# Attention's fill work in a decoder layer: key and value pieces ahead of query pieces, latents loaded one pair per unit, VectorE splitting the key and value weights

## The chip, the cores and the metric

The kernel runs on one core of a Trainium2 chip. The metric is the device time of one execution in microseconds (us); the median of three runs is compared. A profiled execution has a time of its own and a span, from its first to its last instruction.

## The reference, cut to what matters

One layer of a hybrid decoder on 1024 tokens of width 1024, all in float32. A combined input projection feeds two attention mixers and two gates; their gated sum goes through an output projection, then a SwiGLU follows. The mixers have eight heads each:

```python
y_a = _dilated_attention(a_qkv, rel_bias) @ w_up_a            # mixer A, heads 0 to 7
# mixer B: latents c_q (768) and c_kv (256), normalised, expanded per head
q  = einsum('bsl,lhd->bshd', _rmsnorm(c_q,  g_q_lora),  w_uq)   # 8 heads x (64 + 32)
kv = einsum('bsl,lhd->bshd', _rmsnorm(c_kv, g_kv_lora), w_ukv)  # 8 heads x (64 + 64)
q_nope, q_rope = q[..., :64], _rope(q[..., 64:], positions)
k_nope, v = kv[..., :64], kv[..., 64:];  k_rope = _rope(k_r, positions)
# causal softmax((q_nope k_nope + q_rope k_rope) * scale) v
merged = sigmoid(gate_a) * y_a + sigmoid(gate_b) * (y_b @ w_up_b)
```

The expansions with w_uq, w_ukv and w_up_a are the work that the change reorders.

## The kernel before

Every float32 matrix is kept as a rounded high part and the remainder as a low part, and a product is three matmuls (high times high, high times low, low times high). Making the two parts is a "split": ScalarE casts the high part (line L83), then VectorE or GpSimd subtracts it from the source (L84). `wsplit` does that for the weights of mixer B.

The attention stage follows the input projection (whose matmuls are L220). It is a loop over 64 units: unit u is two blocks of 128 queries of head u // 4, the eight heads of mixer A first. A unit's scores are matmuls (L783) that VectorE reads (L785), ScalarE exponentiates (L790) and normalises (L793, or VectorE at L795); three units later its probabilities are transposed (L805), split into ph and pl (L83, L84) and multiplied with v (L824). The next head's q, k0, k1 and v are loaded on GpSimd's DMA queue (L744 to L746 and L748) and its bias table on SyncE's (L747), once the head before the current one has given its buffers back.

Between the units' matmuls TensorE gets fill work from a generator: `spend` hands out matmuls in proportion to the attention work issued. Up to unit 32 the generator is `fill_a`. Its pieces write one accumulator, tile `acc`, which has one buffer:

- f_uk1, eight key pieces of six matmuls (L892), split into two tiles and stored to mkd (L336, L337);
- f_vb, eight value pieces of six matmuls (L87 to L89), copied to SBUF (L939), split into two tiles of which each is stored to vbd (L944);
- f_uq, twelve query pieces of 18 matmuls (L892). Four of them are rotated (L843 to L848), with two table loads `ev<-cst` each.

The tiles of all of them are called ev and come from one pool of seven buffers. `k_rope`, at unit 1, takes eight of these tiles: for each half of the tokens it loads krr (L882) and two tables (L843, L844), shuffles on VectorE (L845), multiplies and adds on GpSimd (L846 to L848), and stores the parts to krd (L884, L885).

The normalised latents lie in DRAM as nqd0 to nqd5 (query) and nqd6, nqd7 (key and value). `load_n` brings a pair of them into SBUF cells on GpSimd's queue (L874), 512 KB each. The raw weight wuk is loaded into cell 4, which later holds one half of nqd2; wuv and wuq are loaded by SyncE (L855).

A scheduler with a timeline of its own orders the instructions of each engine when the program is built. It may move an instruction ahead of others that were written before it, so the written order alone doesn't say what stands on an engine.

Of the kernel before, what the change touches and what calls it, by code (L numbers as in the profile page):

```python
# [27 lines left out]
T = 1024  # L28
# [16 lines left out]
def layer_kernel(ctx: ExitStack, tc: tile.TileContext, xT, c, pos, relT, wada, bada, gains, gq, gkv,  # L45
# [3 lines left out]
    ACT, DVE, PE, POOL, SP = nc.scalar, nc.vector, nc.tensor, nc.gpsimd, nc.sync  # L49
# [32 lines left out]
    def split(src, hi, lo, eng=DVE):  # L82
        ACT.copy(hi, src)  # L83
        eng.tensor_sub(lo, src, f32(hi))  # L84
# [316 lines left out]
    with ExitStack() as s0:  # L401
# [6 lines left out]
        ssq = [early.tile([P, H], F32, name=f"ssq{i}") for i in range(2)]  # L408
# [77 lines left out]
        for k in range(8):  # L486
# [5 lines left out]
            raw = gwr.tile([P, GW], F32, name="gwraw")  # L492
# [5 lines left out]
            hi = gwr.tile([P, GW + 32], F32R, name="gwh")  # L498
            lo = gwr.tile([P, NGP * P], F32R, name="gwl")
# [13 lines left out]
            for j in range(NGP):  # L513
                s = slice(j * P, j * P + P)
# [205 lines left out]
    with ExitStack() as s2:  # L720
# [15 lines left out]
        v_ins = [None]  # L736
# [116 lines left out]
        def wraw(src, n, t=None):  # L853
            raw = (wf.tile([P, T], F32, name="wraw") if t is None else t)[:, :n]
            ld(raw, src)  # L855
            return raw

        def wsplit(src, n, raw=None):
            raw = wraw(src, n) if raw is None else raw
            if n == T:  # L860
                hi, lo = [wk.tile([P, T], F32R, name=f"wk{l}") for l in range(2)]
            else:
                hi, lo = [wf.tile([P, 768], F32R, name=f"w{l}")[:, :n] for l in range(2)]
            split(raw, hi, lo, POOL)
            return hi, lo

        wcols = lambda w: [t.rearrange("p (k f) -> p k f", f=P) for t in w]
# [3 lines left out]
        def load_n(j):  # L871
            t = [cell(NHOME[j] + l, [P, T]) for l in range(2)]
            for l in range(2):
                ldr(t[l], nqd[j][l])  # L874
            nt[j] = t
# [3 lines left out]
        def k_rope():  # L879
            for hf in range(2):  # L880
                t = EV()
                ld(t[:32], krr[:, hsl[hf]])  # L882
                hi, lo = rope(t, 32, hf)
                st(krd[0][:, hsl[hf]], f32(hi)[:32])  # L884
                st(krd[1][:, hsl[hf]], f32(lo)[:32])  # L885
# [60 lines left out]
        def f_uk1(j, hf):  # L946
            ps = accb()
            yield from gemm3g(ps, cur["uk"], n_act(6), 2, hf, 2 * j)
            qk_out(ps, mkd[j], hf, EV)

        def fill_a():
            small = [f_uk1(j, hf) for j in range(4) for hf in range(2)] + [f_vb(tb) for tb in range(8)]
            big = [f_uq(j, hf) for j in (4, 0, 1, 5, 2, 3) for hf in range(2)]
            pat = cycle("ssq")
            while small or big:
                kind = next(pat)
                src = small if kind == "s" and small or not big else big
                yield from src.pop(0)

        def fill_b():  # L960
            for j in range(8):
# [12 lines left out]
        def open_unit(u):  # L974
# [5 lines left out]
                ld(mtab[0], maskt)  # L980
            units[u] = Unit(heads[idx], I, osum[0], 64 * (idx % 2), idx)

        def others(u):
            idx, I = u // 4, u % 4
            if I == 1 and idx < 15:
                heads[idx + 1] = load_head(*seq[idx + 1], (idx + 1) % 2)
            if u == 1:
                with tc.issue_after(v_ins[0].ins):
                    for j in (0, 1, 3, 4, 5, 2):
                        load_n(j)  # L990
                k_rope()

        DEPTH = 3
        FA, FB = (0, 0.7, 32), (35, 0.38)
# [94 lines left out]
    ssq = [X(), X()]  # L1089
# [162 lines left out]
    for ci in range(NC):  # L1252
        for dd in range(2):
# [7 lines left out]
            if dd == 1 and ci == NC - 1:  # L1261
                tail = []
                for f in (20, 21):
                    raw = cell(next(tcell), dt=F32)
                    raw = [raw[:, 0], raw[:, 1]]
# [12 lines left out]
    raw = WP.tile([P, 16, P], F32, name="Wraw")  # L1278
# [158 lines left out]
```

## Time and profile before

| | |
|---|---|
| median of 3 runs | 1672.65 us (1670.92 to 1677.95) |
| profiled execution, its own time | 1676.03 us |
| its span | 1674.2 us |
| TensorE (PE) busy | 1537.7 us, 92% of the span |
| VectorE (DVE) busy | 1240.5 us, 74% |
| ScalarE (ACT) busy | 829.8 us, 50% |
| GpSimd (POOL) busy | 561.5 us, 34% |
| moved by DMA | 321.92 MB, mean 192 GB/s |

Times in the views are microseconds from the span's start. The attention stage runs from about 440 to 838; unit 32 and the end of `fill_a` lie near 667. In a view by time, a bracket at the end of a line tells how long the engine had been idle before it and what ended that.

### The profile page before, as it was taken

The numbers are of one execution on the slowest core, as the hardware profiler recorded it, in microseconds if no ns is written. First come the engines' busy times: TensorE is split into PE (matmuls) and PEld (weight loads), VectorE is DVE, ScalarE is ACT, GpSimd is POOL, SyncE is SP. The second block draws the span as 40 slices with busy tenths as digits, with TensorE's granted clock in tenths as the row PEclk, the third lists the DMA queues.
The fourth block names the chain that finished last, engine by engine and source line by source line (L and its number), as shares of the span: only waits on it lengthen the run. The fifth ranks groups of instructions, "written<-read, shape, count | busy, mean of one in ns | idle before, by whom it ended". The sixth has DMA issues, their size and how long they took to land.

```text
span 1674.2 us, 22241 instructions
## 1 busy us (share of the span) xinstructions
PE 1537.7 (92%) x7306; PEld 1278.2 (76%) x7306; DVE 1240.5 (74%) x2433; ACT 829.8 (50%) x1631; POOL 561.5 (34%) x515
## 2 busy tenths in 40 slices
PE   4989997999779989999999998989999999899996
PEld 2758786877668778999878876768888887688775
DVE  7986669576368657989866678767777786688887
ACT  5743334444467767878733563434444443222324
POOL 0143524424244546433141134322233222222323
PEclk9989999999879999999999998999999999999997
DMA  9438457558997878766195422554454449866412
GB/s 329 178 119 310 160 188 233 172 165 251 295 223 201 202 186 206 189 164 152 46 345 171 151 100 87 178 203 167 175 187 161 152 160 353 324 247 256 154 51 101
DMA packets 175652, 321.92 MB, mean 192 GB/s; under 512 B 37020, under 2 KB 72524, under 8 KB 170288
## 3 DMA queue, kind: packets, MB, share of 16 engines
q1 hardware_dynamic: 107376, 241.75, 42.2%
q0 software_dynamic: 48000, 42.04, 11.7%
q10 hardware_dynamic: 20160, 36.71, 5.8%
q8 instruction: 58, 0.95, 0.2%
q14 instruction: 58, 0.48, 0.1%
HBM read 222.73 MB, written 102.34 MB: 194 GB/s over the span
## 4 chain that ended last, share of the span: by engine, by line
PE 43%; DVE 8%; DMA 8%; ACT 3%; issue 2%; POOL 1%; ACTq 0%; SPq 0%; DVEq 0%; POOLq 0%
PE bk L220 25%; PE acc L892 3%; PE S L783 3%; PE bk L87 3%; PE bk L88 3%; PE bk L89 3%; PE pv L824 2%; DMA Wraw<-wdown 2%; DVE Wop L84 2%; PE tr L805 2%; DMA vbd<-ev 2%; DMA tod<-x 1%; DVE x L1241 1%; DVE cell L84 1%; DMA actd<-x 1%
## 5 line engine op out<-in xcount | busy, mean ns | idle before, releaser
L220 PE MATMUL bk<-cell,Wop 128*128 128x512 f32 x4056 | 951.5, 396 | 51.5 <-DVE x L233 11.0
L220 PEld LDWEIGHTS bk<-cell,Wop 128*128 128x128 f32 x4056 | 771.8, 191 | 225.1 <-ACT x L163 15.1
L190 POOL TENSOR_TENSOR Wsum<-Wraw 128x512 f32<-128x512 f32 (+1 forms) x120 | 156.4, 1304 | 599.0 <-DVE Wop L84 272.2
L83 ACT CAST Wop<-Wsum 128x512 fp32r<-128x512 f32 (+1 forms) x241 | 130.6, 550 | 198.9 <-PE bk L220 117.3
L83 ACT CAST Wop<-Wraw 128x512 fp32r<-128x512 f32 (+2 forms) x182 | 105.6, 593 | 212.4 <-PE bk L220 75.3
L84 DVE TENSOR_TENSOR Wop<-Wsum,Wop 128x512 fp32r<-128x512 f32 (+1 forms) x241 | 155.3, 653 | 61.1 <-ACT Wop L83 60.6
L84 DVE TENSOR_TENSOR Wop<-Wraw,Wop 128x512 fp32r<-128x512 f32 (+2 forms) x182 | 152.3, 843 | 39.5 <-ACT Wop L83 35.8
L783 PE MATMUL S<-cell,cell 128*128 128x128 f32 (+8 forms) x480 | 119.3, 364 | 9.7 <-DMA cell<-ksd 5.5
L1241 DVE SCALAR_TENSOR_TENSOR x<-bk,modc,x 128x512 f32<-128x512 f32 x140 | 103.5, 744 | 20.1 <-PE bk L220 18.8
L84 DVE TENSOR_TENSOR pl<-tr,ph 128x512 fp32r<-128x512 f32 (+1 forms) x160 | 98.4, 630 | 23.9 <-ACT ph L83 22.9
L790 ACT ACTIVATE P<-P,mx 128x512 f32<-128x512 f32 (+7 forms) x128 | 99.3, 778 | 29.5 <-DVE mx L785 17.6
L892 PE MATMUL acc<-cell,w 128*128 128x512 f32 x408 | 112.0, 402 | 0.1
L190 POOL TENSOR_TENSOR Wsum<-Wraw,Wsum 128x512 f32<-128x512 f32 (+1 forms) x60 | 78.5, 1313 | 68.9 <-DVE Wop L84 66.1
L805 PE MATMUL tr<-ident,P 128*128 128x128 f32 x576 | 94.1, 281 | 5.9 <-ACT P L793 5.3
L163 ACT COPY x<-bk 128x512 f32<-128x512 f32 x92 | 52.7, 588 | 91.0 <-PE bk L220 48.1
L87 PE MATMUL bk<-cell,Wop 128*128 128x512 f32 (+1 forms) x240 | 92.3, 385 | 3.7 <-ACT Wop L83 1.9
L824 PE MATMUL pv<-ph,v 128*128 128x256 f32 (+1 forms) x320 | 88.9, 294 | 6.9 <-ACT ph L83 5.6
L783 PEld LDWEIGHTS S<-cell,cell 96*128 96x128 f32 (+1 forms) x480 | 80.8, 196 | 18.6 <-DMA cell<-ksd 5.9
L88 PE MATMUL bk<-cell,Wop 128*128 128x512 f32 (+1 forms) x240 | 91.7, 383 | 0.0
L83 ACT CAST ph<-tr 128x512 fp32r<-128x512 f32 (+1 forms) x160 | 83.3, 545 | 16.3 <-PE tr L805 13.5
L89 PE MATMUL bk<-cell,Wop 128*128 128x512 f32 (+1 forms) x240 | 90.3, 379 | 0.0
L824 PE MATMUL pv<-pl,v 128*128 128x256 f32 x320 | 83.0, 294 | 4.5 <-DVE pl L84 4.1
(255 smaller groups left out, 2221.1 us busy)
## 6 DMA issues: line engine op xcount, KB each, us to landing
tod<-x ACTq DMA_DIRECT2D x140, 256.0 KB, 2.9
cell<-tod SPq DMA_DIRECT2D x70, 512.0 KB, 6.8
Wraw<-win SPq DMA_DIRECT2D x18, 1024.0 KB, 6.6
Wraw<-wgate SPq DMA_DIRECT2D x11, 1024.0 KB, 5.5
Wraw<-wup SPq DMA_DIRECT2D x11, 1024.0 KB, 6.0
Wraw<-wdown SPq DMA_DIRECT2D x20, 512.0 KB, 6.6
ada<-wada SPq DMA_DIRECT2D x16, 512.0 KB, 6.1
cell<-ksd POOLq DMA_DIRECT2D x16, 512.0 KB, 21.4
```

The costliest lines, as they stand in the source:

```text
L83: ACT.copy(hi, src)
L84: eng.tensor_sub(lo, src, f32(hi))
L87: PE.matmul(ps, w[0], a[0], start=first, stop=False)
L88: PE.matmul(ps, w[0], a[1], start=False, stop=False)
L89: PE.matmul(ps, w[1], a[0], start=False, stop=last)
L190: POOL.tensor_tensor(t, a, b, op=op)
L220: PE.matmul(ps, w[:, wi, k], t[k][:, ti], start=start and k == 0 and n == 0, stop=k == self.nk - 1 and n == 2, skip_group_check=True)
L783: anchor[0] = PE.matmul(s, q[:, i * P:i * P + P], k[:, c * wd:c * wd + wd], start=pi == 0, stop=pi == len(passes) - 1)
L805: anchor[0] = PE.transpose(tr[:, co:co + P], self.p[a][:, kb * P:kb * P + P], ident)
L824: anchor[0] = PE.matmul(pv[:, o if l else 0:], v[:, kk], p[:, l:r], start=kk == 0 and n == 0, stop=last and l > 0 and n == 1, skip_group_c ...
L892: PE.matmul(ps, w[wi][:, k0 + k], act(k, ai, hf), start=k == 0 and n == 0, stop=k == nk - 1 and n == 2)
L1241: DVE.scalar_tensor_tensor(xs, self.bk[name], modc[:, 40 + j:41 + j], xs, op0=OP.mult, op1=OP.add)
```

## The change

Three edits. `fill_a` hands out all key pieces, then all value pieces, then the query pieces; before it took two key or value pieces and one query piece in turn. The six query latents are no longer loaded at unit 1 after that head's v load, but one pair in each of the units 2, 3, 4, 6, 7 and 8. The two weights of 1024 columns, wuk and wuv, have their low part made by VectorE and no longer by GpSimd.

```diff
@@ -861,7 +861,7 @@
                 hi, lo = [wk.tile([P, T], F32R, name=f"wk{l}") for l in range(2)]
             else:
                 hi, lo = [wf.tile([P, 768], F32R, name=f"w{l}")[:, :n] for l in range(2)]
-            split(raw, hi, lo, POOL)
+            split(raw, hi, lo, DVE if n == T else POOL)
             return hi, lo
 
         wcols = lambda w: [t.rearrange("p (k f) -> p k f", f=P) for t in w]
@@ -951,11 +951,8 @@
         def fill_a():
             small = [f_uk1(j, hf) for j in range(4) for hf in range(2)] + [f_vb(tb) for tb in range(8)]
             big = [f_uq(j, hf) for j in (4, 0, 1, 5, 2, 3) for hf in range(2)]
-            pat = cycle("ssq")
-            while small or big:
-                kind = next(pat)
-                src = small if kind == "s" and small or not big else big
-                yield from src.pop(0)
+            for g in small + big:
+                yield from g
 
         def fill_b():
             for j in range(8):
@@ -980,15 +977,16 @@
                 ld(mtab[0], maskt)
             units[u] = Unit(heads[idx], I, osum[0], 64 * (idx % 2), idx)
 
+        NU = {2: 0, 3: 1, 4: 3, 6: 4, 7: 5, 8: 2}
+
         def others(u):
             idx, I = u // 4, u % 4
             if I == 1 and idx < 15:
                 heads[idx + 1] = load_head(*seq[idx + 1], (idx + 1) % 2)
             if u == 1:
-                with tc.issue_after(v_ins[0].ins):
-                    for j in (0, 1, 3, 4, 5, 2):
-                        load_n(j)
                 k_rope()
+            if u in NU:
+                load_n(NU[u])
 
         DEPTH = 3
         FA, FB = (0, 0.7, 32), (35, 0.38)
```

What that does to GpSimd's order, at the place behind the last loads for head 1: before, the loads of the query latents (cells 0 to 11, nqd), with the subtraction for wuk (L84, wk1) among them, and behind them the loads for the third head (L744 to L746).

```order
L874 DMA cell8_3982<-nqd4_102 128x1024
L874 DMA cell9_3983<-nqd4_102 128x1024
L84 TENSOR_TENSOR wk1_3915<-cell4_3912,wk0_3914 128x1024
L874 DMA cell10_3986<-nqd5_103 128x1024
L874 DMA cell11_3987<-nqd5_103 128x1024
L874 DMA cell4_3990<-nqd2_100 128x1024
L745 DMA cell21_4238<-ksd1_76 128x1x1024
L744 DMA cell20_4237<-qsd1_72 128x1x1024
L746 DMA cell22_4239<-ksd1_76 128x1x1024
```

After the change the same place reads:

```order
L874 DMA cell8_4362<-nqd4_102 128x1024
L874 DMA cell9_4363<-nqd4_102 128x1024
L874 DMA cell10_4429<-nqd5_103 128x1024
L874 DMA cell11_4430<-nqd5_103 128x1024
L874 DMA cell4_4505<-nqd2_100 128x1024
L745 DMA cell21_4234<-ksd1_76 128x1x1024
L744 DMA cell20_4233<-qsd1_72 128x1x1024
L746 DMA cell22_4235<-ksd1_76 128x1x1024
```

The subtraction is gone from this queue. The loads of the query latents have not been spread over the units; they still stand in one row ahead of the third head's loads.

SyncE's queue at the start of the attention stage, before: the last gate stores (god), k_rope's loads for both halves (krr, cst), two weights wuq, and the third head's bias table rxx2 (L747).

```order
L399 DMA god14_120<-x_3851 128x512
L882 DMA ev_3994<-krr_90 32x512
L843 DMA ev_3996<-cst_130 128x1x512
L844 DMA ev_3997<-cst_130 128x1x512
L882 DMA ev_4009<-krr_90 32x512
L843 DMA ev_4011<-cst_130 128x1x512
L844 DMA ev_4012<-cst_130 128x1x512
L855 DMA wraw_4109<-wuq 128x768
L747 DMA cell23_4241<-rxx2_135 128x1024
L855 DMA wraw_4627<-wuq 128x768
```

And after:

```order
L399 DMA god14_120<-x_3851 128x512
L882 DMA ev_3970<-krr_90 32x512
L843 DMA ev_3972<-cst_130 128x1x512
L844 DMA ev_3973<-cst_130 128x1x512
L747 DMA cell23_4237<-rxx2_135 128x1024
L882 DMA ev_3985<-krr_90 32x512
L843 DMA ev_3987<-cst_130 128x1x512
L844 DMA ev_3988<-cst_130 128x1x512
L855 DMA wraw_4412<-wuv 128x1024
L855 DMA wraw_4871<-wuq 128x768
```

The bias table, which waits until head 0's scores have been read, now stands ahead of the second half's three loads; and the whole of wuv stands ahead of the first wuq.

GpSimd's part of the value pieces, one row for each of a piece's two tiles (L84, `128x4x64`), before, with the split of query pieces (L79, L80) between them:

```order
L84 TENSOR_TENSOR ev_5066<-ev_5064,ev_5066 128x4x64
L84 TENSOR_TENSOR ev_5070<-ev_5064,ev_5070 128x4x64
L748 DMA v_5238<-vad2_93 128x8x128
L84 TENSOR_TENSOR ev_5113<-ev_5111,ev_5113 128x4x64
L84 TENSOR_TENSOR ev_5117<-ev_5111,ev_5117 128x4x64
L84 TENSOR_TENSOR cell15_5157<-osum_4423,cell14_5156 128x256
L79 CAST ev_5277<-ev_5275 128x512
L80 TENSOR_TENSOR ev_5275<-ev_5275,ev_5277 128x512
L745 DMA cell21_5561<-ksd3_78 128x1x1024
L744 DMA cell20_5560<-qsd3_74 128x1x1024
```

And after:

```order
L84 TENSOR_TENSOR ev_4461<-ev_4459,ev_4461 128x4x64
L84 TENSOR_TENSOR ev_4465<-ev_4459,ev_4465 128x4x64
L84 TENSOR_TENSOR ev_4529<-ev_4527,ev_4529 128x4x64
L748 DMA v_4954<-vad2_93 128x8x128
L84 TENSOR_TENSOR ev_4533<-ev_4527,ev_4533 128x4x64
L84 TENSOR_TENSOR ev_4586<-ev_4584,ev_4586 128x4x64
L84 TENSOR_TENSOR ev_4590<-ev_4584,ev_4590 128x4x64
L84 TENSOR_TENSOR cell15_5201<-osum_4433,cell14_5200 128x256 x2
L745 DMA cell25_5280<-ksd2_77 128x1x1024
L744 DMA cell24_5279<-qsd2_73 128x1x1024
L746 DMA cell26_5281<-ksd2_77 128x1x1024
L84 TENSOR_TENSOR ev_4645<-ev_4643,ev_4645 128x4x64
```

Now the tiles of eight value pieces follow each other with only attention's own rows between them. On TensorE, from the first value piece's first matmul to the last one's, 126 attention matmuls stand between the eight pieces, 18 to a gap; before, a query piece of 18 matmuls and its attention work also stood between each pair.

## Rows read from the trace of the kernel before

**Rows 1.** The page: the line of the span.
```profile
span 1674.2 us, 22241 instructions
```

**Rows 2.** Busy time by stretch: PE, PEld, DVE, ACT, POOL; clock, DMA share, GB/s.
```profile
440.00:500.00 60.00, 39.49 (x189) 32.77 (x189) 34.28 (x113) 34.45 (x74) 24.37 (x25) 0.78 1.06 262
...
670.00:840.00 170.00, 167.62 (x1100) 152.99 (x1099) 149.41 (x443) 133.22 (x293) 55.76 (x81) 1.00 0.58 141
```

**Rows 3.** TensorE in order of time: start, us, what, idle before and its end.
```profile
449.62 0.80 PE L892 MATMUL acc<-cell,wk 128*128 128x512 f32 x1 [7.93 <-POOL wk L84]
...
471.93 0.58 PE L824 MATMUL pv<-pl,v 128*128 128x256 f32 x1 [3.59 <-DVE pl L84]
```

**Rows 4.** TensorE in order of time, third head's first scores.
```profile
496.02 0.47 PE L783 MATMUL S<-cell,cell 128*128 128x128 f32 x1 [5.29 <-DMA cell<-ksd]
```

**Rows 5.** TensorE in order of time, while value pieces run.
```profile
594.57 0.77 PE L824 MATMUL pv<-ph,v 128*128 128x256 f32 x2 [1.57 <-ACT ph L83]
...
627.82 1.97 PE L805 MATMUL tr<-ident,P 128*128 128x128 f32 x8 [5.04 <-ACT P L793]
```

**Rows 6.** GpSimd in order of time.
```profile
447.21 2.35 POOL L84 TENSOR_TENSOR wk<-cell,wk 128x1024 fp32r<-128x1024 f32 x1
...
460.62 0.81 POOL L746 DMA_DIRECT2D cell<-ksd  x1
...
467.31 1.26 POOL L847 TENSOR_TENSOR ev<-ev 32x512 f32<-32x512 f32 x1 [4.57 <-DVE P L795]
468.65 1.25 POOL L848 TENSOR_TENSOR ev<-ev 32x512 f32<-32x512 f32 x1
```

**Rows 7.** VectorE in order of time.
```profile
439.98 0.69 DVE L386 TENSOR_TENSOR x<-bk,x 128x512 f32<-128x512 f32 x1 [2.03 <-PE bk L220]
...
459.47 0.67 DVE L785 CUSTOM_DVE_ANT_0 P<-S,cell 128x512 f32<-128x512 f32 x1
...
469.94 0.01 DVE L845 LOAD_MASK_SELECT ev<-ev  x1 [2.65 <-POOL ev L848]
...
470.79 0.49 DVE L795 TENSOR_SCALAR P<-P,mx 128x512 f32<-128x512 f32 x1
471.19 0.68 DVE L84 TENSOR_TENSOR pl<-tr,ph 128x512 fp32r<-128x512 f32 x1
```

**Rows 8.** ScalarE in order of time, the two weight casts.
```profile
438.05 1.05 ACT L83 CAST wk<-cell 128x1024 fp32r<-128x1024 f32 x1 [5.63 <-DMA cell<-wuk]
...
478.26 0.83 ACT L83 CAST w<-wraw 128x768 fp32r<-128x768 f32 x1 [5.18 <-DMA wraw<-wuq]
```

**Rows 9.** SyncE's queue in order of time.
```profile
443.33 0.56 SPq L844 DMA_DIRECT2D ev<-cst  x1
...
447.92 8.33 SPq L855 DMA_DIRECT2D wraw<-wuq  x1
460.18 0.34 SPq L747 DMA_DIRECT2D cell<-rxx  x1
```

**Rows 10.** VectorE's groups, shapes apart: count, busy, mean ns, idle before.
```profile
L84 DVE TENSOR_TENSOR Wop<-Wraw,Wop 128x1024 fp32r<-128x1024 f32 x18 | 23.9, 1330 | 2.9 <-ACT Wop L83 2.2
```

**Rows 11.** ScalarE in order of time, value pieces.
```profile
559.48 0.59 ACT L939 COPY ev<-acc 128x512 f32<-128x512 f32 x1
...
560.53 0.71 ACT L83 CAST ev<-ev 128x256 fp32r<-128x256 f32 x2
...
624.32 0.40 ACT L83 CAST ev<-ev 128x256 fp32r<-128x256 f32 x1 [6.67 <-DMA vbd<-ev]
```

**Rows 12.** GpSimd in order of time, value pieces.
```profile
561.02 1.44 POOL L84 TENSOR_TENSOR ev<-ev 128x256 fp32r<-128x256 f32 x2 [1.31 <-ACT ev L83]
```

**Rows 13.** DMA issues of this stretch: count, KB, median us to landing.
```profile
vbd<-ev SPq DMA_DIRECT2D x16, 256.0 KB, 8.4
```

**Rows 14.** The chain of waits in order of time, its two longest pieces here.
```profile
579.21 14.51 DMA vbd<-ev
...
611.80 12.44 DMA vbd<-ev
```

## What is predicted, and why

> **What bounds the kernel now.** I read the busy time by stretch first: which stretch of the attention stage is not paced by TensorE? From 670 to 840 us TensorE is busy 167.62 of 170 us; no edit can win anything there. From 440 to 500 us it is busy 39.49 of 60, at a granted clock of 0.78, while the DMA share is 1.06 [rows 2]. So the stage starts with its transfers full and its matmul engine waiting. Then TensorE in order of time, for its waits of over 3 us. There are four: 7.93 us up to 449.62 for wuk's low part, 3.59 up to 471.93 for VectorE, 5.29 up to 496.02 for the third head's keys, and 5.04 up to 627.82 for ScalarE [rows 3 to 5]. For each I followed the engine that it names to what held that one.
>
> The first: ScalarE had the high part at 439.10, but GpSimd's subtraction (2.35 us) began at 447.21, because it stands in GpSimd's queue among the latent loads [rows 6, 8]. The second: VectorE stood at k_rope's second shuffle, which began at 469.94 after a wait for GpSimd's addition L848; that one came right behind L847, which started at 467.31 [rows 6, 7]. The row puts L847's wait down to VectorE, but its other input is the table load issued at 443.33 [rows 9]. I take this load, 24 us under way, as the cause. The third: the load was issued at 460.62 and landed by 496.02, 35.4 us later [rows 4, 6]. The fourth: ScalarE had waited 6.67 us for a buffer that a store of a value piece still held; the store took 12.44 us to land [rows 11, 14].
>
> So one wait of the four is GpSimd's own. The other three end with a transfer, and the change has to be judged by when transfers start.
>
> **The change part by part.** *wuk on VectorE.* The price stands in VectorE's rows: 18 subtractions of 1024 columns, mean 1.33 us [rows 10]. The cast ends at 439.10, so the low part is there at 440.4. Two additions L386 stood ahead of the first score read and now come behind the subtraction; the last ran from 439.98 for 0.69 us [rows 7]. With 0.6 us for each (estimate from that row) it ends near 441.6, 1.0 us later. TensorE then waits about 1.4 us where it waited 7.93: **-6.5 us**. What would exclude more: its next scores need VectorE's read. wuv's subtraction costs VectorE 1.33 us once. The cast (1.05, as for wuk) and it make 2.4 us, behind which 32 attention matmuls stand ahead of the first value piece. At 0.152 us each (167.62 us for 1100 [rows 2]) these cover 4.9 us: nothing, and 2.4 us if that cover were gone. GpSimd is relieved of the same two subtractions; no wait hangs on it after 447: nothing.
>
> *The latent loads.* In the built order they have not moved, so this edit by itself is worth nothing. But the order of SyncE's queue did change around it: head 2's bias table now stands ahead of k_rope's second half, and it waits until head 0's scores are read. That was done at 460.1 [rows 7]; 6.5 us earlier is 453.6. k_rope's second loads, issued by 447.92 before [rows 9], now leave behind 453.6.
>
> *Given back at k_rope.* The first table still lands near 467, so L848 still ends near 470. VectorE reaches the second shuffle 6.5 us earlier, less some 1.5 us of its own work which the new order puts ahead of the shuffle (reciprocals, and operations like the 0.49 and 0.68 us [rows 7]). So 5 of the 6.5 us are waited here: **+5 us**; 0 if that load comes 5 us earlier too, 6.5 if nothing hides.
>
> *ScalarE's cast for the first wuq.* It waited to 478.26 for a load issued at 447.92 [rows 8, 9]. ScalarE's casts of ph and its exponentials stand behind it. Now the load leaves after 453.6 behind 1 MB of bias table and wuv. If it needs its 30 us again it lands near 487, +8.7; if the stretch moves its bytes at the old rate, the half column of wuv more (128 KB, 0.5 us at 262 GB/s [rows 2]) is all, and VectorE's extra work ahead makes it -1. I take **+2 us**, near the low end, because the share of 1.06 says that the rate, not the time of issue, sets the landing.
>
> *Head 2's keys.* Their issue waits for head 0's scores and comes 6.5 us earlier, so 35.4 us end at 489.5, ahead of the 490.7 at which TensorE asked: **-5.3 us**; 0 if the landing stays.
>
> *Value pieces in a row.* Before, these cost TensorE 1.57 and 5.04 us [rows 5]; they leave that place: **-6.6 us**. In the new place: a piece holds its copy from 559.48 to 562.46, when GpSimd's two subtractions end, 3.0 us [rows 11, 12]. Each of its two tiles is held from the cast (560.53) some 1.6 us to the store, and then until that lands, L. Seven buffers make T = (3.0 + 2 x (1.6 + L)) / 7 us per piece. TensorE offers a piece every 24 matmuls (6 and 18), 3.6 us at 0.152. With the median L of 8.4 us [rows 13] T is 3.3 and nothing is lost; with 12.44 it is 4.4, with 14.51 it is 5.0 [rows 14], for eight pieces +6.6 and +11.4 us. Pieces now queue four deep, so I take the upper of the ordinary landings, 12.44: **+6.6 us**.
>
> The other stalls and the clock I leave as they are; 39.49 us at 0.78 would be 30.8 at full clock, so up to 8.7 us could come back if the waits went.
>
> Sum: -6.5 + 5 + 2 - 5.3 - 6.6 + 6.6 = -4.8 us. The profiled execution took 1676.03 us (span 1674.2 [rows 1]), so 1671.2 like for like; its median is 3.4 us lower, so the forecast is **1668 us**, -0.3%.
>
> **A rule against the change.** The rows show a DMA share of 1.06 at 262 GB/s while both SyncE's and GpSimd's queues have loads waiting [rows 2, 9]. The Trainium skill, DMA: Bandwidth & Descriptors, section Issuing engines are not separate DMA queues, says that all issuing engines' transfers run on the same 16 DMA engines and interleave. By that rule alone nothing that reorders issues shortens the stretch. The trace agrees as far as the share of 1.06 goes; its time is worked out as the second rival.
>
> **The rivals.** *Faster.* Either the table load comes earlier with its competitors (terms +5 and +2 fall to 0, sum -11.8, 1661 us), or the stores land in the median 8.4 us (+6.6 falls to 0, sum -11.4, 1661). Both: -18.4, 1654. For the first speaks that GpSimd's queue is 2.35 us shorter; for the second that 8.4 is the median [rows 13]; against both, the share of 1.06 and the 14.51 us with two pieces in flight.
>
> *Bound by transfers.* The stretch up to 496 ends when its bytes have moved, wherever TensorE waits: the first four terms sum to 0, the value pieces to -6.6 + 6.6, and the time stays at 1673. For it: the share. Against it: it falls to 0.58 later [rows 2], and 7.93 us are a pure queue wait.
>
> *Slower, by one mechanism:* the stores of value pieces. If four pieces in flight make each landing 20 us (14.51 with fewer [rows 14]), T is 6.6 and eight pieces lose 24 us: -4.8 - 6.6 + 24 = +12.6, 1685 us. Its sign turns against us beyond 8.4 us, which needs T of 6.1, a landing of 18.2 us.
>
> **How the numbers follow.** About 0.5%, 8.4 us, is what a measurement of this kernel can tell from no change. Forecast 0.28 and transfer-bound 0.18 make "same" 0.46; the faster rival has 0.33 and the slower one 0.21. The low end is the sum with both faster cases and 2 us of clock, 1652; the high end is the slower rival with a third of the +8.7 that the cast can cost more, 1688. The likeliest case's own range is 1662 to 1676.
>
> **What would show it.** Right: TensorE's wait for wk falls to 1 to 2 us; a new wait of 7 to 10 us for VectorE before 472, with VectorE at L845 behind L848; ScalarE waits for wuq until 478 to 483; no wait over 1 us for head 2's keys; value pieces end to end in 30 to 40 us, ScalarE waiting there for vbd stores; no 5 us wait near 628. Wrong: L847 starts before 463, or the casts for wuq wait beyond 487, or landings of vbd above 18 us, or the time is out by what the clock does in those gaps.

## The result, and the profile after

| | median, us | ratio to before, 95% interval | first scores to first L87 of the next stage, us |
|---|---|---|---|
| before | 1674.89 | | 399.1 |
| changed | 1688.05 | 1.0056 [1.0032, 1.0079] | 414.8 |

The change made the kernel slower, by a little more than the 0.5% taken as the bound, where 1668 was forecast. The medians are of five runs each; their quotient is 1.0079, at the upper end of the interval, so the size of the loss lies between some 9 us (by the ratio) and 13 us (by the medians). The profiled execution took 1688.63 us; its page begins:

```profile
span 1686.8 us, 22217 instructions
...
PE 1540.7 (91%) x7306; PEld 1278.0 (76%) x7306; DVE 1249.9 (74%) x2435; ACT 828.3 (49%) x1631; POOL 557.0 (33%) x513
```

TensorE's busy time is 3.0 us more than before; 12.6 us of span were added [rows 1]. To see where, take TensorE's first scores (L783) and the first matmul of the stage behind attention (L87), by time. Before:

```profile
439.78 0.33 PE L783 MATMUL S<-cell,cell 128*128 128x128 f32 x2
...
838.87 0.58 PE L87 MATMUL bk<-cell,Wop 128*128 128x512 f32 x1 [1.87 <-ACT Wop L83]
```

After:

```profile
443.87 0.33 PE L783 MATMUL S<-cell,cell 128*128 128x128 f32 x2
...
858.68 0.50 PE L87 MATMUL bk<-cell,Wop 128*128 128x512 f32 x1 [1.86 <-ACT Wop L83]
```

Attention is 15.7 us longer, the part ahead of it 4.1 us longer and the part behind it 7.2 us shorter. The last two lie within the scatter of single executions: over those profiled here the first scores came between 436.6 and 443.9 us, and the part behind lasted 828.0 to 835.9; the kernel before alone gave 835.3 and, in a second execution, 832.3. So the stage has to explain the result. TensorE's waits from 435 to 870 us by what ended them (total, times, longest), before:

```profile
PE acc L892 <- POOL wk L84: 7.9, 1, 7.9
PE pv L824 <- ACT ph L83: 5.6, 4, 1.8
PE S L783 <- DMA cell<-ksd: 5.5, 2, 5.3
PE tr L805 <- ACT P L793: 5.3, 2, 5.0
PE pv L824 <- DVE pl L84: 4.1, 3, 3.6
```

After:

```profile
PE pv L824 <- DVE pl L84: 12.7, 9, 10.0
PE S L783 <- DMA cell<-ksd: 10.4, 1, 10.4
PE acc L892 <- ACT ev L903: 9.0, 1, 9.0
PE acc L87 <- ACT ev L939: 5.9, 3, 2.3
PE acc L892 <- DVE ev L84: 3.2, 2, 2.8
PE pv L824 <- ACT ph L83: 2.7, 2, 2.5
```

With the smaller rows the waits add to 36.6 us before and 50.9 after: 14.3 of the 15.7 us. Read row by row: the wait for wk is gone, and so is the 5.04 us wait of [rows 5]. In their place stand two waits of 10 us at the start of the stage, 5.9 us at the value pieces, and 9.0 us at a place that the prediction doesn't have. (The wait for wk became two short waits for latents, together 2.1 us.) The single events, by time:

```profile
445.27 0.47 PE L892 MATMUL acc<-cell,wk 128*128 128x512 f32 x1 [1.06 <-DMA cell<-nqd]
...
477.36 0.58 PE L824 MATMUL pv<-pl,v 128*128 128x256 f32 x1 [10.02 <-DVE pl L84]
...
502.66 1.01 PE L783 MATMUL S<-cell,cell 128*128 128x128 f32 x3 [10.36 <-DMA cell<-ksd]
...
606.92 6.12 PE L892 MATMUL acc<-cell,w 128*128 128x512 f32 x18 [9.00 <-ACT ev L903]
```

**The start.** VectorE stood at the second shuffle, and its load was late. VectorE and then SyncE, by time:

```profile
476.00 0.01 DVE L845 LOAD_MASK_SELECT ev<-ev  x1 [9.79 <-DMA ev<-krr]
```

```profile
457.96 0.34 SPq L747 DMA_DIRECT2D cell<-rxx  x1
458.34 0.43 SPq L882 DMA_DIRECT2D ev<-krr  x1
```

The 64 KB of krr were issued behind head 2's bias table and were there 17.7 us later.

**The rotated pair.** What SyncE itself waited for from 575 to 602 us, and the chain that ended last:

```profile
SPq L843 <- DMA vbd<-ev: 10.8, 1, 10.8
SPq L844 <- DMA vbd<-ev: 4.7, 1, 4.7
```

```profile
578.23 0.40 POOL cell L746
...
580.25 17.66 DMA ev<-cst
...
604.86 0.72 DVE ev L845 x2
```

GpSimd and then ScalarE, by time:

```profile
598.14 1.26 POOL L846 TENSOR_TENSOR ev<-ev 128x512 f32<-128x512 f32 x1 [16.95 <-DMA ev<-cst]
```

```profile
604.85 0.62 ACT L83 CAST ev<-ev 128x512 fp32r<-128x512 f32 x1 [13.10 <-POOL ev L848]
```

The query phase begins with the rotated pieces of j = 4. Their first table load left right behind head 6's loads (L744 to L746 until 578.23, bias table 578.18, 512 KB each) and took 17.66 us; GpSimd stood still for it. The second half's two table loads waited 15.5 us on SyncE for tiles that the last value pieces' stores still held; this wait lay beside the first table's and is not on the chain. The next, plain query piece's copy (L903) stands on ScalarE behind the first half's cast, so TensorE waited 9.0 us for the accumulator, and its clock fell: from 564 to 634 us it was busy 58.35 of 70 us at a granted 0.90, before in the like stretch 61.77 at 0.98. The windows (PE busy first, granted clock third from the end), after and then before:

```profile
564.00:634.00 70.00, 58.35 (x322) 50.63 (x321) 38.05 (x109) 40.57 (x89) 35.04 (x36) 0.90 0.66 172
```

```profile
560.00:630.00 70.00, 61.77 (x360) 53.03 (x359) 42.66 (x134) 48.77 (x113) 32.38 (x38) 0.98 0.73 187
```

As busy time times clock that is 52.5 against 60.5 us of work at full clock.

### The profile page after: what moved, and what is told of

Same layout as the page of the kernel before. It is cut to its first block, busy times and chain, and to the rows that moved or that the text cites. A ratio compares the mean times of both kernels' runs of the same rounds, so it can differ in the third digit from the quotient of the medians.

```text
span 1686.8 us, 22217 instructions
## 1 busy us (share of the span) xinstructions
PE 1540.7 (91%) x7306; PEld 1278.0 (76%) x7306; DVE 1249.9 (74%) x2435; ACT 828.3 (49%) x1631; POOL 557.0 (33%) x513
## 3 DMA queue, kind: packets, MB, share of 16 engines
q0 software_dynamic: 48000, 42.04, 11.8%
## 4 chain that ended last, share of the span: by engine, by line
PE 56%; DMA 17%; DVE 16%; issue 4%; ACT 4%; POOL 2%; SPq 0%; ACTq 0%; DVEq 0%; POOLq 0%
PE bk L220 34%; PE acc L892 4%; PE S L783 3%; PE bk L87 3%; PE bk L88 3%; PE pv L824 3%; PE bk L89 3%; DVE Wop L84 3%; DMA cell<-nqd 2%; DMA cell<-ksd 2%; PE tr L805 2%; DMA Wraw<-wdown 2%; DVE cell L84 2%; DMA cl<-wada 1%; DMA ev<-cst 1%
## 5 line engine op out<-in xcount | busy, mean ns | idle before, releaser
L84 DVE TENSOR_TENSOR Wop<-Wsum,Wop 128x512 fp32r<-128x512 f32 (+1 forms) x241 | 155.3, 652 | 65.1 <-ACT Wop L83 64.3
L84 DVE TENSOR_TENSOR Wop<-Wraw,Wop 128x512 fp32r<-128x512 f32 (+2 forms) x182 | 153.4, 850 | 43.1 <-ACT Wop L83 41.1
L783 PE MATMUL S<-cell,cell 128*128 128x128 f32 (+8 forms) x480 | 119.7, 366 | 12.7 <-DMA cell<-ksd 10.4
L84 DVE TENSOR_TENSOR pl<-tr,ph 128x512 fp32r<-128x512 f32 (+1 forms) x160 | 98.0, 630 | 15.5 <-ACT ph L83 14.5
L790 ACT ACTIVATE P<-P,mx 128x128 f32<-128x128 f32 (+7 forms) x128 | 99.3, 779 | 18.3 <-DVE mx L785 9.9
L783 PEld LDWEIGHTS S<-cell,cell 96*128 96x128 f32 (+1 forms) x480 | 81.1, 198 | 21.9 <-DMA cell<-ksd 10.5
L87 PE MATMUL bk<-cell,Wop 128*128 128x512 f32 (+1 forms) x240 | 91.1, 380 | 3.3 <-ACT Wop L83 1.9
L892 PEld LDWEIGHTS acc<-cell,w 128*128 128x128 f32 x408 | 76.4, 193 | 21.9 <-ACT ev L903 9.2
L88 PE MATMUL bk<-cell,Wop 128*128 128x512 f32 (+1 forms) x240 | 90.6, 378 | 0.0
```

Of the source, the lines that this page charges most:

```text
L87: PE.matmul(ps, w[0], a[0], start=first, stop=False)
L88: PE.matmul(ps, w[0], a[1], start=False, stop=False)
L783: anchor[0] = PE.matmul(s, q[:, i * P:i * P + P], k[:, c * wd:c * wd + wd], start=pi == 0, stop=pi == len(passes) - 1)
L790: ACT.activation(t[:, :n], t[:, :n], AF.Exp, bias=mx[:, 0:1], scale=-1.0, accum_out=mx[:, 1:2])
L892: PE.matmul(ps, w[wi][:, k0 + k], act(k, ai, hf), start=k == 0 and n == 0, stop=k == nk - 1 and n == 2)
```

## The experiments

"Stage" is first scores to first L87 in the profiled execution. Medians are of 12 runs (e6_apart and e20_late_mix 6, e9_evp8 7, e8_rope_first 11); each ratio is to the runs of the kernel before that were taken with that kernel. A line number can differ by some lines from one kernel to the next.

| run | median, us | ratio, 95% interval | stage, us |
|---|---|---|---|
| e1_split | 1668.36 | 0.9959 [0.9944, 0.9974] | 398.5 |
| e5_order | 1674.90 | 0.9987 [0.9968, 1.0007] | 400.9 |
| e3_plain_first | 1672.55 | 1.0002 [0.9984, 1.0021] | 407.6 |
| e6_apart | 1687.54 | 1.0075 [1.0050, 1.0101] | 414.4 |
| e7_no_tables | 1679.96 | 1.0031 [1.0013, 1.0049] | 406.7 |
| e8_rope_first | 1684.47 | 1.0040 [1.0018, 1.0061] | 412.9 |
| e10_wuk_only | 1680.61 | 1.0025 [1.0006, 1.0045] | 406.0 |
| e14_late | 1683.19 | 1.0036 [1.0011, 1.0061] | 408.8 |
| e9_evp8 | 1685.51 | 1.0071 [1.0046, 1.0097] | 408.4 |
| e18_late_evp8 | 1680.43 | 1.0024 [1.0000, 1.0048] | 406.8 |
| e19_mix | 1683.65 | 1.0053 [1.0035, 1.0071] | 408.1 |
| e20_late_mix | 1686.38 | 1.0076 [1.0047, 1.0104] | 407.6 |
| before_again | 1678.62 | 1.0011 [0.9991, 1.0031] | 399.2 |
| e1_again | 1669.35 | 0.9968 [0.9946, 0.9991] | 397.0 |
| e24_direct | 1676.81 | 1.0006 [0.9987, 1.0025] | 403.0 |
| e25_split_direct | 1673.44 | 0.9991 [0.9969, 1.0012] | 399.1 |
| e27_late_direct | 1671.47 | 0.9977 [0.9963, 0.9991] | 398.5 |

**One edit at a time.** The third edit has no run of its own: the first two together, with the latents loaded at unit 1 as before, are built into the same order of instructions on all five engines as the changed kernel. The first edit alone (e1_split):

```diff
-            split(raw, hi, lo, POOL)
+            split(raw, hi, lo, DVE if n == T else POOL)
```

> The kernel before with the first edit alone: VectorE splits wuk and wuv, the fill keeps its two-small-one-big pattern. Theory A (the new fill order costs the time: 9.0 us at the two rotated query pieces that now stand next to each other, and 6.7 us at the value pieces): nothing of that is here, TensorE's 7.93 us wait for wk falls to about 1.5, so about 1668 us, ratio 0.996. Theory B (the start of the stage costs it: the second rotation on VectorE waits some 10 us for its krr load, and head 2's keys are waited for 10.4 us): SyncE's queue has a query weight ahead of the second krr load, so a part of both is here, 1672 to 1680 us, ratio 0.998 to 1.003. Theory C (VectorE's splits in themselves slow the stage or its clock): ratio about 1.005.

And the second alone (e5_order), `for g in small + big: yield from g`:

> The kernel before with the second edit alone: key and value pieces first, GpSimd still splits wuk. Theory A: the waits at the value pieces (6.7 us against 6.6 before) and at the rotated query pieces (9.0 us) are here, and the 7.9 us wait for wk stays: about 1684 to 1690 us, ratio 1.005 to 1.009. Theory B: the second half's krr load is not behind head 2's bias table, so VectorE does not wait 10 us and head 2's keys cost about 5 us as before: 1673 to 1678 us, ratio 0.999 to 1.002. Theory C: ratio about 1.000.

The split gains 0.4%, as theory A has it; the order comes out even, as only B and C have it; the two together lose 0.6%. So each theory is right for one run alone, and what costs time is neither edit but their meeting. The start of the stage hardly sets the changed kernel apart from e1_split, though that one is faster: there krr was issued 5.4 us after the first scores in place of 14.5, was there at 31.4 in place of 32.1, and TensorE waited nearly as long, 9.5 and 7.6 us in place of 10.0 and 10.4 (by time):

```profile
469.95 0.58 PE L824 MATMUL pv<-pl,v 128*128 128x256 f32 x1 [9.51 <-DVE pl L84]
...
493.67 1.01 PE L783 MATMUL S<-cell,cell 128*128 128x128 f32 x3 [7.58 <-DMA cell<-ksd]
```

With the order alone TensorE waited 0.8 us at the rotated pair, though its pieces run in the same sequence: SyncE waited 1.3 us for the stores in place of 15.5, and both halves' tables left by 571.37, 15 us ahead of the next head's loads (586.35). So it may matter where the built order puts the tables and the last stores among the heads' loads.

**Moving the rotated pair.** e3_plain_first and e6_apart:

```diff
-            big = [f_uq(j, hf) for j in (4, 0, 1, 5, 2, 3) for hf in range(2)]
+            big = [f_uq(j, hf) for j in (0, 4, 1, 5, 2, 3) for hf in range(2)]
```

```diff
-            for g in small + big:
+            for g in small[:12] + big[:1] + small[12:14] + big[1:2] + small[14:] + big[2:]:
```

> The changed kernel with query pieces in the order 0, 4, 1, 5, 2, 3: a plain pair ahead of the rotated pair. Theory A, if the 9.0 us wait comes from the rotated pair following the value pieces' stores and not from the pair itself: the wait falls below 3 us, about 1680 us, ratio to the kernel before 1.001 to 1.003; if the two rotated halves standing next to each other are enough (eight buffers wanted, seven there), the wait stays at 6 us or more and the ratio at 1.005. Theory B: nothing changes at the start of the stage, ratio 1.005.

> The changed kernel with the two halves of the first rotated query piece pulled forward among the last value pieces: value pieces 0 to 3, first half, value pieces 4 and 5, second half, value pieces 6 and 7, then the rest. Theory A: the two halves no longer want their buffers at once, and their table loads have value pieces to lie beside, so the 9.0 us wait falls below 3 us: about 1680 us, ratio to the kernel before 1.001 to 1.003. Theory B: ratio 1.005 as for the changed kernel.

With a plain pair first the whole loss is gone by the medians, though TensorE still waited 5.8 us at the rotated pair behind it, for the second half's copy (L907):

```profile
604.82 6.40 PE L892 MATMUL acc<-cell,w 128*128 128x512 f32 x18 [5.81 <-ACT ev L907]
```

Its stage is 8.5 us longer than before's all the same. Pulled among the value pieces, the 9.0 us wait fell to 1.5 us in two, but the stage stayed as long: waits of 2 to 3 us for osum, mx, ph and P came instead, and the ratio is 1.0075. The forecast for e6_apart missed; a wait that is moved is not a wait that is gone. The two runs also say that the kernel's time does not follow the wait at the pair alone.

**What the pair waits for.** e7_no_tables has `POOL.memset(cs, 1.0)` and `POOL.memset(sn, 0.0)` for the two table loads, e10_wuk_only has `DVE if n == T and "uk" not in cur else POOL`, and e8_rope_first puts head 2's bias table behind k_rope's loads:

```diff
-                ld(u, dap(rxx[hd], 127, [[REXT - 1, P], [1, T]]))
+                if hd == 2:
+                    with tc.issue_after(sn_ins[0].ins):
+                        ld(u, dap(rxx[hd], 127, [[REXT - 1, P], [1, T]]))
```

> The changed kernel with the query pieces' rotation tables not loaded: GpSimd fills the two table tiles with constants, so the query part of the rotation is left out of the result. Theory R (the first rotated pair waits because its table loads stand in SyncE's and GpSimd's queues behind the next head's 512 KB loads, which the two earlier edits only do together): the 9.0 us wait of TensorE for the rotated pieces' eviction goes, and the low clock behind it; about 1677 to 1681 us, ratio to the kernel before 1.000 to 1.003. Theory S (the loss lies at the start of the stage: the second rotation behind head 2's bias table, head 2's keys 5 us later): no more than 2 us come back, ratio 1.004 to 1.006.

> The changed kernel with the value weight's split back on GpSimd: VectorE splits wuk alone. In the built order head 2's bias table still stands ahead of the second rotation's loads, but the first rotated query pair's tables now stand ahead of the next head's loads. Theory R: the rotated pair no longer waits 9 us; about 1676 to 1680 us, ratio to the kernel before 1.000 to 1.003. Theory S: the start is as in the changed kernel and so is the time, ratio 1.005 to 1.008.

> The changed kernel with head 2's bias table held back on SyncE's queue until the second half's rotation loads are issued. Theory R: nothing changes at the rotated query pieces, ratio to the kernel before 1.005 to 1.008. Theory S: the second half's loads are issued about 10 us earlier, VectorE's 9.8 us wait and TensorE's 10.0 us behind it go, about 1676 to 1680 us, ratio 1.001 to 1.003. If the stage's first 56 us are set by its transfers (head 2's keys came 56.2 to 58.8 us after the first scores in four kernels with different queues), the wait only moves to head 2's keys and the time stays: ratio 1.004 to 1.008.

Without any table, GpSimd (by time) still waited for the stores before it could fill the second half's tiles, and TensorE still lost 6.0 us:

```profile
585.26 0.53 POOL L844 MEMSET ev<- 128x512 f32 x1 [7.32 <-DMA vbd<-ev]
...
588.12 0.53 POOL L845 MEMSET ev<- 128x512 f32 x1 [2.33 <-DMA vbd<-ev]
```

```profile
595.39 5.78 PE L896 MATMUL acc<-cell,w 128*128 128x512 f32 x18 [5.98 <-ACT ev L907]
```

So tiles alone can cost 6.0 us there, and tables are not all of it: theory R had the wait go, and 1.0031 lies just outside its range. How the changed kernel's 9.0 us divide is not shown, since its chain goes through the first half's table. In e10_wuk_only the start is as in the changed kernel, and the rotated pair differs; its waits at SyncE and at TensorE:

```profile
SPq L843 <- DMA vbd<-ev: 1.4, 1, 1.4
```

```profile
PE acc L892 <- ACT ev L903: 0.5, 1, 0.5
```

TensorE also waited 1.6 us there for the second half's copy (L907). Three of its four tables left from 573.98 to 576.70, ahead of the head loads at 584.58 to 588.00, the fourth at 586.48. Theory R holds for the place, and 1.0025 is in its range, though its interval overlaps that of the changed kernel. In four kernels with the new order the two go together: 15.5 us at SyncE and 9.0 at TensorE in the changed kernel, 15.0 and 8.1 in e8_rope_first, 1.4 and 2.1 here, 1.3 and 0.8 in e5_order.

e8_rope_first tells the other half. SyncE, VectorE and TensorE, by time:

```profile
444.44 0.84 SPq L887 DMA_DIRECT2D ev<-krr  x1
```

```profile
471.30 0.01 DVE L850 LOAD_MASK_SELECT ev<-ev  x1 [10.15 <-DMA ev<-krr]
```

```profile
496.09 1.01 PE L788 MATMUL S<-cell,cell 128*128 128x128 f32 x3 [8.16 <-DMA cell<-ksd]
```

The load left 5.2 us after the first scores (439.22) in place of 14.5, and was there 32.1 us after them, as in the changed kernel. The place in the queue was not what set it, and the time hardly moved: S falls, the third forecast (set by transfers) holds.

**Transfers at the start.** e14_late moves the six latent pairs behind head 2's keys:

```diff
-        NU = {2: 0, 3: 1, 4: 3, 6: 4, 7: 5, 8: 2}
+        NU = {5: 0, 6: 1, 7: 3, 8: 4, 9: 5, 10: 2}
...
+                kl = ldr(k1, dap(ksd[j], (P + r) * T, [[0, 2], [T, 64], [1, T]]))
+                if hd == 2:
+                    k_ins[0] = kl
...
-                load_n(NU[u])
+                with tc.issue_after(k_ins[0].ins):
+                    load_n(NU[u])
```

> The changed kernel with the six query-latent pairs held back on GpSimd's queue until head 2's keys are issued, so that the spreading the change writes is really there (in its built order no load had moved). Theory T (the first 56 us of the stage are set by its transfers, so the wk wait that VectorE's split removes only moves to the second rotation and to head 2's keys): with some 6 MB taken out of this stretch, at the 274 GB/s moved there worth about 22 us of transfers, VectorE's 9.8 us and TensorE's 10.0 us and 10.4 us waits there fall below 3 us each; TensorE gains 8 to 15 us, so 1673 to 1680 us, ratio to the kernel before 0.998 to 1.003. Theory R alone (all of the loss lies at the rotated query pieces): waits move, time stays, ratio 1.004 to 1.006.

VectorE reached the second shuffle at 455.44 without a wait, 17.6 us after the first scores, and head 2's keys were there. But the latents now lay in front of head 3 (TensorE, by time):

```profile
515.50 0.44 PE L785 MATMUL S<-cell,cell 128*128 128x128 f32 x1 [5.36 <-DMA cell<-qsd]
...
519.10 0.48 PE L785 MATMUL S<-cell,cell 128*128 128x128 f32 x1 [3.16 <-DMA cell<-ksd]
```

And at the start TensorE now waited for the low parts of key pieces, whose tiles come from the same pool (435 to 870 us; totals):

```profile
PE acc L894 <- DVE ev L84: 11.5, 2, 6.1
```

So the stage won 6.0 of the 8 to 15 us, and 1.0036 lies below theory R's range and above theory T's.

**More buffers, or pieces spread out.** e9_evp8 gives e8_rope_first `pool(s2, "evp", 8)` and `bufs=1` for tmp; e18_late_evp8 gives e14_late the same.

> The kernel of the last batch that holds head 2's bias table back (1684.5 us, ratio 1.0040), with eight eviction buffers in place of seven (the space comes from a second copy buffer that is given up). Theory B (the rotated pair waits for buffers: with no tables to load its second half still waited 7.3 and 2.3 us for the value pieces' stores, and TensorE 6.0 us): TensorE's wait for the rotated eviction falls from 8.1 to below 3 us, and its waits for the value pieces' evictions from 7.6 to about 5; 1674 to 1679 us, ratio 0.999 to 1.002. If the tables' own landing is what counts, the wait stays at 6 us or more, ratio 1.003 to 1.005.

> The changed kernel with both: query latents behind head 2's keys, and eight eviction buffers. Theories T and B together: 1662 to 1670 us, ratio 0.992 to 0.997, below the kernel with VectorE's splits alone (0.9959) only if the value pieces' own cost shrinks too. If one theory falls, 1673 to 1680 us.

Both missed. In e9_evp8 the rotated wait fell only from 8.1 to 5.5 us, and waits of 6.5 us for a key piece's low part and 3.5 us for v came up; in e18_late_evp8, whose time lies at the edge of the range for one theory fallen, one of 12.1 us for v (vad). Both also give up a tmp buffer and are ordered otherwise from the first loads on, so they don't tell the buffer's worth. e19_mix and e20_late_mix hand out value and query pieces by turns (the second with the latents at unit 5, behind head 2's keys):

```diff
-            for g in small + big:
+            mix = [g for p in zip(small[8:], big) for g in p]
+            for g in small[:8] + mix + big[8:]:
```

> The changed kernel, keys first as there, but then value and query pieces by turns, one of each, query pieces in the order 0, 4, 1, 5, 2, 3. Theory V (in every kernel with the new order TensorE does about 7 us less work than before between 60 and 140 us of the stage, because eight value pieces in a row bring 16 splits and 16 stores of 256 KB, whose buffers the evictions wait for; spread out, the stores have query pieces to lie beside): 5 to 7 us of that come back and the rotated pair stays apart from them, so 1673 to 1678 us, ratio to the kernel before 0.998 to 1.002. If the start of the stage alone sets what is lost, or the cost follows the value pieces wherever they stand: 1679 us or more, ratio 1.003 to 1.006.

> The same mixed order, and the query latents behind head 2's keys on GpSimd's queue. Theories V and T together: 1666 to 1672 us, ratio 0.994 to 0.998. If the held-back latents only move the wait to the next head, as in the run with late latents (head 3's queries and keys waited 8.6 us there), no better than the mixed order alone.

Theory V fell, and e20_late_mix missed the range for V and T together by 14 us; it was no better than the mixed order alone, as its other forecast had it. In e19_mix TensorE waited 6.6 us for the copy of one value piece among query pieces, because ScalarE waited 8.05 us for a vbd store. So in this kernel it was not the pieces' density that counted; a single store that was late was enough.

**The value pieces without their copy**, and two repeats:

```diff
-            ev = EV()
-            ACT.copy(ev, ps)
...
-                pv = ev[:, g * 256:g * 256 + 256].rearrange("p (h d) -> p h d", d=64)
-                split(pv, v[:, :, 0], v[:, :, 1], POOL)
+                pv = ps[:, g * 256:g * 256 + 256].rearrange("p (h d) -> p h d", d=64)
+                split(pv, v[:, :, 0], v[:, :, 1], DVE)
```

> The changed kernel with the value pieces split straight from their sums (ScalarE and VectorE read PSUM; no copy into an eviction buffer, two buffers a piece in place of three, GpSimd's 16 splits go to VectorE). Theory B2 (buffers held by the value pieces' stores cost the 7 us there and most of the wait at the first rotated pair): TensorE's waits for the value pieces fall from 6.7 us to below 2, that for the rotated pair from 9.0 to below 4; 1674 to 1679 us, ratio 0.999 to 1.003. If VectorE, which takes on 16 splits of some 0.5 us, or TensorE's single accumulator, which is held longer, is the next limit: 1684 us or more.

> VectorE's splits alone with the old fill order, and the value pieces split straight from their sums. If buffers cost time there too (TensorE waited 2.6 us for the value pieces and 3.2 us at 627 behind them): 1664 to 1667 us, ratio 0.992 to 0.995. If not, as the splits alone, 0.996.

> The kernel before against itself: ratio 1.000, interval within 0.003 of it. Its second profiled execution gives the scatter of a stage's length: attention took 399.1 us and the stages behind it 835.3 us in the first; if they come out more than 2 us away, a difference of this size between single executions means nothing.

> VectorE's splits alone, a second time: ratio 0.994 to 0.998 if the first measurement holds. If the split gains in the attention stage, that stage is 3 us or more shorter than in the second execution of the kernel before; if the stage's start is set by transfers (theory T), head 2's keys come 56 to 57 us after the first scores again and the stage is as long as in the kernel before within 1 us.

In e24_direct TensorE's waits at those two places (500 to 620 us; totals) are

```profile
PE acc L87 <- DVE ev L84: 2.9, 3, 1.2
PE acc L892 <- ACT ev L903: 2.7, 2, 2.4
```

in place of 6.7 and 9.0, so 10.1 us less, and the stage is 11.8 us shorter: theory B2 holds but for the value pieces, where 2.9 us stayed of a forecast "below 2", and 1.0006 is about the change without its new cost. This run also parts the tables from the stores. SyncE and then GpSimd, by time:

```profile
588.09 0.61 SPq L843 DMA_DIRECT2D ev<-cst  x1
```

```profile
596.74 1.29 POOL L846 TENSOR_TENSOR ev<-ev 128x512 f32<-128x512 f32 x1 [8.14 <-DMA ev<-cst]
```

The first table left right behind head 6's loads (585.35 to 587.30) here too, but it was there 8.65 us later in place of 17.66. The last stores had left ahead of those loads (by 586.15), and SyncE waited 3.7 us for stores in place of 15.5. So a table behind the heads' loads is not enough for the 9.0 us. The edit also takes 16 subtractions from GpSimd and eight copies from ScalarE; what that is worth beside the tiles is not shown. With the old order the same edit gains nothing (e25_split_direct: 0.9991 against 0.9959, in neither of its two forecasts). The kernel before against itself gave 1.0011, its stage 399.2 us; head 2's keys came 58.7 us after the first scores where they had come after 56.2, so a difference of 2.5 us at one place means nothing. The splits alone gave 0.9968, a stage of 397.0; neither forecast for that stage came out (3 us or more shorter, or as long within 1 us), and head 2's keys came at 55.6.

**Both remedies** (e27_late_direct: e14_late and e24_direct together):

> Value pieces split straight from their sums, and the six query-latent pairs held back behind head 2's keys. Theory T (the start's transfers are a cost of their own, some 4 to 6 us net of what moves to head 3): 1667 to 1672 us, ratio to the kernel before 0.995 to 0.998. If holding them back only moves the wait from one head to the next: 1674 to 1679 us, ratio 0.999 to 1.002, as without it (1.0006).

0.9977 where e24_direct has 1.0006, in theory T's range, though TensorE waits 11.3 us for head 3's queries now. That the transfers at the start are a cost of their own is likely and not shown: holding the latents back changed the ratio by -0.0029 here, by -0.0020 from the changed kernel to e14_late and by +0.0023 from e19_mix to e20_late_mix, and each of these pairs of intervals overlaps. The splits alone have the lowest ratios measured, 0.9959 and 0.9968, and are faster than the kernel before and the changed one; the interval of e27_late_direct overlaps theirs.

## Why the prediction was wrong

*wuk on VectorE, -6.5 us.* Right at its place: TensorE's 7.93 us became 1.06 and 0.99 us for latents. The price of 1.33 us was 1.23. The 1.4 us that the term left waiting had no row behind it: TensorE asked at 441.69 [rows 3], after the 440.4 forecast for the low part.

*Given back at k_rope, +5, and head 2's keys, -5.3.* **Head 2's keys are the term that failed by most at the start**: "35.4 us end at 489.5" took the landing as fixed from the issue, and the issue as 6.5 us earlier. They were issued only 1.5 us earlier in the stage (L746 at 463.24, behind latent loads that reached to 458.46) and were there 39 us later: 10.36 us in place of 5.29 [rows 4], a cost of 5.1 us where 5.3 were to be gained. The wait for pl grew from 3.59 [rows 3] to 10.02, 6.4 us given back: within the bounds of 0 to 6.5, but for krr, not for L848. The four terms of the start summed to -4.8 us. Head 2's keys came 55.5 to 59.2 us after the first scores in every kernel in which the latents stood ahead of them, wherever the wk wait was. That is the second rival, bound by transfers, which had 0.18; its sum of 0 for these terms was the nearest of those stated. In the profile the wk wait had lain beside the transfers' time and its removal uncovered it: from 444 to 504 us after, TensorE was busy 32.29 us at 0.78, 25.2 us at full clock, against 30.8 [rows 2].

*ScalarE's cast of wuq, +2 us.* It ran at 485.20, 41.3 us after the first scores; before 38.5 [rows 8]. Right in size; no wait of TensorE is put down to it.

*Value pieces, -6.6 and +6.6 us.* Right in size: the 5.04 us wait is gone, and in the new place TensorE waited 5.9 and 0.8 us, 6.7. The reason fits in part. Two stores on the chain took about the 12.44 us that the sum had taken:

```profile
538.91 12.01 DMA vbd<-ev
...
558.08 11.14 DMA vbd<-ev
```

But of ScalarE's two waits for a tile at the copies (L939) only one ended with a value piece's store (3.17 us up to 569.29); the other ended with a key piece's (2.25 us up to 547.26). That 6.6 was met to 0.1 us is partly luck. And the 8.4 us of [rows 13], called the median landing, stands on two of sixteen stores, of 4.4 and 12.4 us: the view has no landing for the others.

*The step that failed behind the start* is a term put at nothing: "The other stalls and the clock I leave as they are". "Seven buffers make T ..." counts the seven tiles among value pieces alone. The same pool serves who comes next, and the next are two rotated halves with eight tiles and four table loads. The last stores left at 579.84 and 581.61, right behind 2 MB for head 6, and SyncE's waits for stores ended at 593.64 and 598.95; the first table left at 580.25 and was there 17.66 us later. The slower rival had part of the mechanism (tiles held by these stores) and nearly the time (1685), but at the value pieces, and with landings of 20 us where those on the chain took 12.01 and 11.14; that its time came near is luck. The rotated pieces have no term in the sum. They cost 9.0 us and the low clock behind it in the profile, and this wait is down to 2 or 3 us in the run with fewer tiles held (e24_direct, 1.0006) and in that with the tables ahead (e10_wuk_only, 1.0025). That the pair makes the whole loss is not shown: e3_plain_first loses nothing with 5.8 us waited there, and e6_apart loses as much as the change with 1.5.

With 0 for the start, 0 for the value pieces and 9.0 for the pair, 1673 becomes 1682; the remaining 6 us of the median (2 us by the ratio) I don't divide: the clock is in them (58.35 busy us at 0.90 in place of 0.98 are 4.7 us of work less), and the scatter of the parts around the stage.

What stays open: in profiled executions the splits alone shorten the stage by only 0.6 and 2.2 us, while the medians give 6 us. The parts around the stage were together 4.5 to 6.1 us shorter in both (1269.0 and 1269.4 us against 1275.1 and 1273.9). Over all executions they scatter from 1267 to 1275, so the profiles can't place the gain. By the medians the wk wait's removal is then worth nearly the 6.5 us forecast; by the waits in the profile almost all of it is given back within the start. Which holds is open.

## What to carry to other kernels

A wait on a queue that lies beside full DMA engines may not be worth its length: before pricing its removal, look how long after the stage's start the next loads land, and in what that time changes. When pieces of work are reordered, count the tiles of a shared pool across the seam between two kinds of pieces, stores still under way included. And two edits of which each is harmless can be a loss together where a scheduler then puts small loads and stores behind large loads; measure them apart.

## What the runs showed of the hardware

A load of 64 KB took 26.9 us (e8_rope_first, 444.44 to 471.30) or 17.7 us (changed kernel) and was there at the same 32.1 us of the stage, while the DMA share was 1.06 to 1.09; with the latents out of the way it was there 17.6 us into the stage at the latest. Issuing it 9.3 us earlier in the stage did not help. The Trainium skill, DMA: Bandwidth & Descriptors, section Issuing engines are not separate DMA queues, has all engines' transfers share 16 DMA engines; these rows agree, as moving GpSimd's latent loads brought forward this load of SyncE's. Two stores of value pieces took 12.01 and 11.14 us on the changed kernel's chain; the last two, right behind 2 MB of loads, seem to have taken 13.8 and 17.3 us, from their issue to the ends of SyncE's waits for stores.
